# Transposes of the normed rows two token tiles later, and two units' first products ahead of the last transposes, in a hybrid encoder layer

## The chip, the core and the metric

One core of a Trainium2 chip runs the whole kernel. Its engines are TensorE (PE: matmuls and transposes; the loads of its stationary operand are shown as PEld), VectorE (DVE), ScalarE (ACT), GpSimd (POOL) and SyncE (SP, which here only issues DMAs). Each engine takes its instructions in order; semaphores tie the engines together. The metric is the device time of one execution in microseconds (us), as the median over runs.

## What is computed

One encoder layer on 2304 tokens (256 of a prompt and 2048 of a sample) with a model width of 1024: a norm, an input projection, an RWKV group and an attention group, an output projection, and a gated feed-forward net. The part that matters here is the end of the layer:

```
def rms_norm(x, g):
    y = xf * lax.rsqrt(jnp.mean(xf * xf, axis=-1, keepdims=True) + NORM_EPS)
    return (y * g.astype(jnp.float32)).astype(x.dtype)
...
    x = x + jnp.concatenate([y_rwkv, y_att], axis=-1) @ w_out
    h = rms_norm(x, norm2_g)
    x = x + (jax.nn.silu(h @ ffn_gate) * (h @ ffn_up)) @ ffn_down
    return x
```

The feed-forward width is 2816, that is 22 columns of 128. All data is fp32. A product of two fp32 operands is made of three matmuls: each operand is split into a high and a low part (`hi`, `lo`), and hi·hi, hi·lo and lo·hi are added up in PSUM.

## The kernel before, in words

The kernel runs the input projection, the RWKV phases and the attention first (the last store of the attention is issued at 2293.49 us of the profiled execution). Then `out_ffn` is called three times, for three blocks of 768 tokens, in the order 1, 0, 2 of `FF_ORDER`. It is the only function that the change touches. A block goes through these stages:

- Output projection, first half of the columns (0 to 511): six token tiles of 128 rows, 8 k-tiles each, `part` at lines 991 to 994; line 1000 adds the sum to the residual rows `xw`.
- Output projection, second half of the columns, one token tile after the other (loop over `j`, lines 1046 to 1071). One tile is 24 matmuls of 128x512 (lines 211 to 213). Its rows are then added to the residual (DVE, line 1050), stored (DMA on POOL's queue, line 1051), squared and summed (ACT, line 193), brought to the reciprocal root (POOL, lines 160 and 161), and multiplied by it and by the gain (DVE, line 1058). The result `h`, 128 tokens by 1024, is transposed on PE in 8 pieces of 128x128 (line 1062), because the feed-forward products need the width on the partitions, and ACT copies the pieces from PSUM (line 1063) into the four tiles `B` (names `cg` in the profile): two halves of the width by two halves of the tokens, each 128 x 4 x 384.
- The operands. The gate and up products are done with 7 products in place of 8 for each pair of columns: `b11` and `b21` are tiles of `B` as they are, `t1` to `t4` are differences of such tiles (`sub`, line 1073 and the following lines), and `b22` is the last tile. Each is split into `hi` (ACT) and `lo` (DVE) by `op` into two `H` buffers. `t1` and all later operands need all six token tiles; `b11` and `b21` need only the first three.
- 22 units (`units`): gate and up of 11 pairs of columns. A unit is 7 products of 12 matmuls of 128x384 (line 1087), with the operands b11, b21, t1, t2, b22, t3, t4 in this order. Its weights are two raw tiles of 128x1024 (`wsr`, loaded by SP), sums of their quarters (`sw`: POOL lines 1025 and 1035, DVE lines 1034 and 1039), and their splits (`wsh`, `wsl`, 4 buffers; `w2h`, `w2l`, 2 buffers). The generator `weights(u + 1)` is advanced one step after each product of unit `u`. The sum of products 1, 4 and 6 stays in one PSUM tile, which ACT copies out (lines 1113, 1122, 1128) before the next product is added to it; the copies go into `c`, one of the four `cg` buffers, so that the first unit's `c` has to wait until a tile of `B` is used up. 
- The down projection and the final norm.

The program is built with a scheduler that places the instructions of each engine by a model of its own; the order that a program really has is therefore shown as rows of the built program where it matters.

## Time and profile before

| | us |
|---|---|
| median of 3 runs (lowest to highest) | 4184.22 (4174.27 to 4196.87) |
| the profiled execution, its own time | 4194.28 |
| its span from the first to the last instruction | 4192.2 |
| PE busy | 3935.4 (94%) |
| DVE, ACT, POOL busy | 2867.8, 2010.2, 1252.0 |
| mean granted TensorE clock | 0.96 |

The clock is given as a share of 2.4 GHz; its two levels are 1.2 and 2.4 GHz. Times in the rows further down count from the start of the span. A row of the timeline gives the start, the length, the engine, the line, the operation, what is written and read, its size, how many equal instructions the row merges, and in brackets the idle time before it and what ended it. A row of a stretch gives its bounds and length, then for PE, PEld, DVE, ACT and POOL the busy time and the number of instructions, the granted clock, the share of the DMA engines' time and GB/s.

### The profile page before, as it was taken

To read this page: it belongs to the slowest core of one execution; us is meant where nothing else is said; L and a number is where in the kernel's file an instruction comes from. 1 tells how busy PE (TensorE), PEld (TensorE's weight loads), DVE (VectorE), ACT (ScalarE), POOL (GpSimd) and SP (SyncE) were. 2 spreads that over 40 slices of the span, in tenths; PEclk is the share of its full clock that TensorE was granted. 3 is DMA by queue.
4 is the path that set the end of the run, shared out by engine and by line. 5 is a ranking of instruction groups with operands and counts; after the bars stand their busy time and mean duration, and the time that the engine had idled before them with its cause. 6 is when DMAs were issued, how large, how long until landed. Compare 5 with 4: busy or idle time off the path is not lost.

```text
span 4192.2 us, 71175 instructions
## 1 busy us (share of the span) xinstructions
PE 3935.4 (94%) x26208; PEld 3379.6 (81%) x26208; DVE 2867.8 (68%) x4553; ACT 2010.2 (48%) x3940; POOL 1252.0 (30%) x1776
## 2 busy tenths in 40 slices
PE   8999999889999999999998789999799999799998
PEld 7987888657777787777775689988689988599987
DVE  5478686899889767898876377745377745377743
ACT  5354444456666555656665244434244433244432
POOL 2255353533233657443433012200122200112200
PEclk9999999879999999999999899999899999899999
DMA  6576566652434444444431323353223243222341
GB/s 202 164 213 210 182 209 197 203 139 46 113 68 99 103 107 113 104 109 111 108 83 48 123 96 101 96 182 122 109 91 106 103 174 130 96 100 102 101 171 70
DMA packets 646876, 524.32 MB, mean 125 GB/s; under 512 B 368512, under 2 KB 555520, under 8 KB 646528
## 3 DMA queue, kind: packets, MB, share of 16 engines
q1 hardware_dynamic: 577264, 438.36, 35.0%
q0 software_dynamic: 16944, 68.43, 4.9%
q10 hardware_dynamic: 52320, 12.98, 1.4%
q8 instruction: 207, 3.39, 0.3%
q14 instruction: 141, 1.16, 0.1%
HBM read 355.59 MB, written 166.37 MB: 125 GB/s over the span
## 4 chain that ended last, share of the span: by engine, by line
PE 78%; DVE 9%; POOL 3%; DMA 3%; issue 3%; ACT 3%; SPq 1%; ACTq 0%; DVEq 0%; POOLq 0%
PE acc L1087 23%; PE acc L211 9%; PE acc L212 9%; PE acc L213 9%; PE at L913 4%; PE g L657 3%; PE ao L917 3%; PE ao L916 3%; PE as L880 3%; PE as L881 2%; DVE nm L882 1%; DVE ptl L181 1%; PE hb L730 1%; PE hb L733 1%; PE hb L705 1%
## 5 line engine op out<-in xcount | busy, mean ns | idle before, releaser
L1087 PE MATMUL acc<-H,wsh 128*128 128x384 f32 x3168 | 814.5, 338 | 12.1 <-ACT cg L1113 12.1
L1087 PEld LDWEIGHTS acc<-H,wsh 128*128 128x128 f32 x3168 | 580.3, 191 | 13.4 <-ACT cg L1113 13.1
L1087 PE MATMUL acc<-H,wsl 128*128 128x384 f32 x1584 | 534.1, 337 | 0.0
L901 POOL TENSOR_SCALAR p<-p,f 128x512 f32<-128x512 f32 (+1 forms) x528 | 371.6, 725 | 287.9 <-DVE f L897 238.9
L211 PE MATMUL acc<-wsh,H 128*128 128x512 f32 x1080 | 432.8, 403 | 14.1 <-ACT wsh L175 14.1
L884 ACT ACTIVATE p<-as,nm 128x512 f32<-128x512 f32 (+1 forms) x528 | 360.5, 683 | 158.9 <-DVE nm L882 127.8
L212 PE MATMUL acc<-wsl,H 128*128 128x512 f32 x1080 | 431.1, 399 | 0.0
L213 PE MATMUL acc<-wsh,H 128*128 128x512 f32 x1080 | 425.8, 399 | 0.0
L175 ACT CAST pth<-at 128x512 fp32r<-128x512 f32 x520 | 299.7, 585 | 241.1 <-PE at L913 235.4
L181 DVE TENSOR_TENSOR ptl<-at,pth 128x512 fp32r<-128x512 f32 x520 | 353.0, 682 | 80.4 <-ACT pth L175 78.3
L882 DVE TENSOR_REDUCE nm<-as 128x1 f32<-128x512 f32 (+1 forms) x528 | 352.6, 673 | 77.4 <-PE as L881 74.8
L211 PE MATMUL acc<-hThi,wih 128*128 128x384 f32 x1008 | 351.5, 349 | 0.8 <-ACT hThi L175 0.7
L212 PE MATMUL acc<-hTlo,wih 128*128 128x384 f32 x1008 | 348.3, 346 | 0.0
L213 PE MATMUL acc<-hThi,wil 128*128 128x384 f32 x1008 | 348.0, 345 | 0.0
L913 PE MATMUL at<-ident,p 128*128 128x128 f32 x2080 | 329.5, 279 | 2.9 <-POOL p L901 2.5
L181 DVE TENSOR_TENSOR wsl<-wsr,wsh 128x1024 fp32r<-128x1024 f32 x156 | 193.0, 1237 | 195.1 <-ACT wsh L175 194.7
L175 ACT CAST wsh<-wsr 128x1024 fp32r<-128x1024 f32 x156 | 164.1, 1052 | 333.7 <-PE acc L213 162.3
L913 PEld LDWEIGHTS at<-ident,p 128*128 128x128 f32 x2080 | 264.7, 143 | 69.1 <-POOL p L901 5.6
L1087 PEld LDWEIGHTS acc<-H,wsl 128*128 128x128 f32 x1584 | 301.2, 190 | 0.0
L1025 POOL TENSOR_TENSOR sw<-wsr 128x512 f32<-128x512 f32 x66 | 84.8, 1285 | 691.2 <-DVE wsl L181 600.3
L880 PE MATMUL as<-kh,qs 128*128 128x512 f32 (+1 forms) x528 | 248.7, 471 | 31.2 <-ACT p L884 26.0
L211 PEld LDWEIGHTS acc<-wsh,H 128*128 128x128 f32 x1080 | 211.4, 196 | 59.1 <-ACT wsh L175 14.8
(661 smaller groups left out, 8379.7 us busy)
## 6 DMA issues: line engine op xcount, KB each, us to landing
wsr<-in_ffn_gate SPq DMA_DIRECT2D x66, 512.0 KB, 3.5
wsr<-in_ffn_up SPq DMA_DIRECT2D x66, 512.0 KB, 3.8
wsr<-in_ffn_down SPq DMA_DIRECT2D x66, 512.0 KB, 3.5
wir<-in_w_in POOLq DMA_DIRECT2D x63, 512.0 KB, 4.5
hd<-hid POOLq DMA_DIRECT2D x66, 384.0 KB, 3.7
H<-hd SPq DMA_DIRECT2D x33, 768.0 KB, 5.6
cl<-ard SPq DMA_DIRECT2D x144, 128.0 KB, 3.0
zT<-z SPq DMA_DIRECT2D x84, 192.0 KB, 2.7
```

Source lines behind the costliest of these rows:

```text
L175: nc.scalar.copy(out=hi, in_=src)
L181: e.tensor_tensor(out=lo, in0=src, in1=hi.bitcast(F32), op=ALU.subtract)
L211: mm(out, ahi, bhi, start=first, stop=False)
L212: mm(out, ahi, blo, start=False, stop=False)
L213: mm(out, alo, bhi, start=False, stop=last)
L657: nc.tensor.matmul(psgs[e][:, q, :], bk[rows, q, :], cl[rows, e, q, :], start=True, stop=True)
L880: nc.tensor.matmul(pss[:, :hw], qs[:, h, :], kh, start=True, stop=False)
L882: dve.tensor_reduce(out=nm[:, h, i:i + 1], in_=pss[:, :hw], axis=AX.X, op=ALU.max, negate=True)
L884: act.activation(out=p_[:, :hw], in_=pss[:, :hw], func=AF.Exp, bias=nm[:, h, i:i + 1], accum_out=ls[:, h, i:i + 1])
L901: pool.tensor_scalar(out=t, in0=t, scalar1=f[:, h, i:i + 1], scalar2=1.0, op0=ALU.mult, op1=ALU.mult)
L913: nc.tensor.transpose(tp[:, h, :], pt[h, i][:, k * P:(k + 1) * P], self.ident)
L1087: nc.tensor.matmul(acc, x[l][:, k, :], y_[r][:, k, :], start=first and k == 0 and i == 0, stop=k == 3 and i == 2, skip_group_check=True)
```

## The change

The diff keeps every matmul, transpose, split and sum of a block and changes their order and some buffers. The transposes of a tile become a function `turn(j)`. In the loop over the tiles `turn(j - 2)` is called after the product of tile `j`, so that the transposes of tile 0 stand behind the product of tile 2; `turn(4)` and `turn(5)` stand behind the loop. `h` now lies in one of the 14 `H` buffers and no longer in one of the four `wsr` buffers, and `load(1)` comes earlier. The unit becomes a class whose `steps()` is a generator with a stop after each product. Behind the loop the first two products of unit 0 (b11, b21) are called before `turn(4)` and `turn(5)`, and the first two of unit 1 before t2 is made; the weights of both units are advanced by hand in between. From unit 2 on the loop is as it was.

```
-            h = RAW()
+            h = HT([P, D], F32)
             dve.scalar_tensor_tensor(out=h, in0=xw[j], scalar=r, in1=g2, op0=ALU.mult, op1=ALU.mult)
-            for q in range(2):
-                tp = ACC().rearrange("p (i t) -> p i t", t=P)
-                for i in range(4):
-                    nc.tensor.transpose(tp[:, i, :], h[:, (q * 4 + i) * P:(q * 4 + i + 1) * P], self.ident)
-                act.copy(out=B[q][t][:, :, jj * P:jj * P + P], in_=tp)
-            if j == 2:
+            hs.append(h)
+            if j >= 2:
+                turn(j - 2)
+            if j == 3:
+                load(1)
+            if j == 4:
+                wts = [weights(0), weights(1)]
+                wt = [next(wts[0])]
                 op("b11", B[0][0])
                 op("b21", B[1][0])
-            if j == 3:
-                wg = weights(0)
-                for wt in wg:
-                    pass
-                load(1)
...
+        u0, u1 = Unit(0, wt[0]), None
+        p0 = u0.steps()
+        next(p0)
+        next(p0)
+        turn(4)
+        turn(5)
+        wt.append(next(wts[1]))
+        (b11, b12), (b21, b22) = B
+        sub = lambda out, x, y_: dve.tensor_tensor(out=out, in0=x, in1=y_, op=ALU.subtract)
+        sub(b11, b12, b11)
+        op("t1", b11)
+        next(wts[0])
+        next(wts[0])
+        u1 = Unit(1, wt[1])
+        u1.g = u0.c
+        p1 = u1.steps()
+        next(p1)
+        next(p1)
+        sub(b12, b22, b12)
+        sub(b11, b22, b11)
+        op("t2", b11)
+        next(p0)
+        next(wts[0])
+        op("b22", b22)
+        next(p0)
+        next(wts[0])
+        op("t3", b12)
+        sub(b21, b21, b11)
+        op("t4", b21)
+        next(wts[0])
+        for _ in p0:
+            next(wts[1], None)
+        load(2)
```

What the scheduler made of it is seen in the built programs. The first place is PE behind the last product of the second half, in the first block: `acc<-ident` are transposes (8 to a tile), L1087 of before and L1082 of the change are the units' products. Before:

```order
L213 MATMUL acc<-wsh,H 128x512
L1062 MATMUL acc<-ident,wsr 128x128 x8
L1087 MATMUL acc<-H,wsh 128x384 x2
L1087 MATMUL acc<-H,wsl 128x384
L1087 MATMUL acc<-H,wsh 128x384 x2
```

Now:

```order
L213 MATMUL acc<-wsh,H 128x512
L1054 MATMUL acc<-ident,H 128x128 x8
L1082 MATMUL acc<-H,wsh 128x384 x2
L1082 MATMUL acc<-H,wsl 128x384
L1082 MATMUL acc<-H,wsh 128x384 x2
L1082 MATMUL acc<-H,wsl 128x384
L1082 MATMUL acc<-H,wsh 128x384 x2
L1082 MATMUL acc<-H,wsl 128x384
L1082 MATMUL acc<-H,wsh 128x384 x2
L1082 MATMUL acc<-H,wsl 128x384
L1082 MATMUL acc<-H,wsh 128x384
L1054 MATMUL acc<-ident,H 128x128 x8
```

Before, the 8 transposes behind the last tile's product are that tile's own, and all products of the units follow. Now they are those of tile 3; a first product of unit 0 follows (its 12 matmuls, and one of the second product), then the transposes of tile 4, the rest of the second product, the transposes of tile 5, the two first products of unit 1, and then the third product of unit 0.

The second place is ACT from the last weights of the output projection on (`wsh<-wsr`, `w2h<-wsr`), in the first block; `junk,ss<-xw` is the squaring of a tile's rows, `cg<-acc` the copy of half of a tile's transposes.

```order
 L175 CAST wsh<-wsr 128x1024 x3
 L175 CAST w2h<-wsr 128x512
-L175 CAST wsh<-wsr 128x1024 x2
+L175 CAST wsh<-wsr 128x1024
+L175 CAST w2h<-wsr 128x512
+L175 CAST wsh<-wsr 128x1024
+L193 ACTIVATE junk,ss<-xw 128x1024 x2
+L1055 COPY cg<-acc 128x4x128
 L193 ACTIVATE junk,ss<-xw 128x1024
-L1063 COPY cg<-acc 128x4x128 x2
+L1055 COPY cg<-acc 128x4x128 x2
```

Two tiles are squared before the first copy of transposes, where one was; and the cast of unit 1's `w2h` now stands before the cast of the last weights of the output projection.

The third place is DVE from the last tile's multiplication by the gain to the low parts of t2, b22 and t3 (the row with x3), in the first block. `cg<-cg` are the differences of the operands, `H<-cg,H` low parts of operands, `wsl<-sw,wsh` low parts of weights, L1034 and L1039 sums of weights. Before:

```order
L1058 SCALAR_TENSOR_TENSOR wsr<-xw,rstd,gain 128x1024
L1073 TENSOR_TENSOR cg<-cg 128x1536 x2
L181 TENSOR_TENSOR H<-cg,H 128x1536
L1073 TENSOR_TENSOR cg<-cg 128x1536
L181 TENSOR_TENSOR wsl<-sw,wsh 128x1024
L1073 TENSOR_TENSOR cg<-cg 128x1536
L181 TENSOR_TENSOR H<-cg,H 128x1536 x3
```

Now:

```order
L1039 TENSOR_TENSOR sw<-wsr,sw 128x512
L1143 TENSOR_TENSOR cg<-cg 128x1536
L181 TENSOR_TENSOR wsl<-sw,wsh 128x1024
L1143 TENSOR_TENSOR cg<-cg 128x1536
L181 TENSOR_TENSOR H<-cg,H 128x1536
L181 TENSOR_TENSOR wsl<-sw,wsh 128x1024
L1143 TENSOR_TENSOR cg<-cg 128x1536
L1034 TENSOR_TENSOR sw<-sw,wsr 128x512
L1143 TENSOR_TENSOR cg<-cg 128x1536
L1039 TENSOR_TENSOR sw<-wsr,sw 128x512
L181 TENSOR_TENSOR H<-cg,H 128x1536 x3
```

Between the first difference and the low part of t2 there now stand two low parts of weights where there was one, and one pair of weight sums (L1034, L1039: those of unit 2). The pair of unit 1 stands between the last tile's multiplication and the first difference; before, it stood ahead of that multiplication. Ahead of the multiplication DVE now has the low parts of unit 0's and unit 1's first weights, of b11 and of b21. The other two blocks have the same order at these places.

## Rows read from the trace of the kernel before

**Rows 1.** The page, part 1: PE, busy time, share of the span, instructions.

```profile
PE 3935.4 (94%) x26208; PEld 3379.6 (81%) x26208; DVE 2867.8 (68%) x4553; ACT 2010.2 (48%) x3940; POOL 1252.0 (30%) x1776
```

**Rows 2.** Stretches of three blocks and one unit: length, engines' busy times, clock, DMA.

```profile
2347.40:2460.30 112.90, 79.39 (x336) 70.63 (x337) 55.27 (x51) 39.93 (x54) 17.14 (x24) 0.79 0.20 70
2969.40:3085.00 115.60, 81.85 (x336) 72.45 (x337) 55.14 (x51) 39.98 (x54) 17.09 (x24) 0.78 0.20 69
3594.00:3709.60 115.60, 81.53 (x337) 72.18 (x337) 55.29 (x51) 39.92 (x54) 17.10 (x24) 0.78 0.20 69
...
2445.80:2460.30 14.50, 14.50 (x85) 14.50 (x84) 9.49 (x13) 6.84 (x11) 2.54 (x2) 1.00 0.22 72
```

**Rows 3.** What PE waited for, 2338 to 3720 us: total, times, longest.

```profile
PE acc L1062 <- DVE wsr L1058: 89.2, 18, 8.0
PE acc L1087 <- ACT cg L1113: 12.1, 3, 4.0
```

**Rows 4.** Timeline of PE around the transposes of tile 0, first block.

```profile
2342.90 0.39 PE L213 MATMUL acc<-wsh,H 128*128 128x512 f32 x1
...
2346.98 0.39 PE L213 MATMUL acc<-wsh,H 128*128 128x512 f32 x1
2351.60 1.97 PE L1062 MATMUL acc<-ident,wsr 128*128 128x128 f32 x8 [4.23 <-DVE wsr L1058]
2353.22 0.78 PE L211 MATMUL acc<-wsh,H 128*128 128x512 f32 x1
```

**Rows 5.** Timelines of DVE, ACT and POOL: the way of tile 0 to `h`.

```profile
2347.41 0.69 DVE L1050 TENSOR_TENSOR xw<-acc,xw 128x512 f32<-128x512 f32 x1 [1.91 <-PE acc L213]
2348.13 1.06 ACT L193 ACTIVATE junk<-xw 128x1024 bf16<-128x1024 f32 x1 [5.11 <-DVE xw L1050]
2349.65 0.57 POOL L161 TENSOR_TENSOR rstd<-rstd,mhalf 128x1 f32<-128x1 f32 x1
2350.26 1.28 DVE L1058 SCALAR_TENSOR_TENSOR wsr<-xw,rstd,gain 128x1024 f32<-128x1024 f32 x1 [2.16 <-POOL rstd L161]
```

**Rows 6.** Timeline of PE: last transposes, first block; then t2's product.

```profile
2421.02 1.94 PE L1062 MATMUL acc<-ident,wsr 128*128 128x128 f32 x8 [7.97 <-DVE wsr L1058]
...
2434.95 1.01 PE L1087 MATMUL acc<-H,wsh 128*128 128x384 f32 x2 [4.05 <-ACT cg L1113]
...
2440.40 0.34 PE L1087 MATMUL acc<-H,wsl 128*128 128x384 f32 x1
```

**Rows 7.** Timeline of PE in the attention: transposes among other matmuls.

```profile
2289.64 0.60 PE L913 MATMUL at<-ident,p 128*128 128x128 f32 x4
```

**Rows 8.** Timelines of DVE and ACT: first difference to the copy before t2.

```profile
2422.76 3.62 DVE L1073 TENSOR_TENSOR cg<-cg 128x1536 f32<-128x1536 f32 x2 [1.89 <-ACT cg L1063]
...
2429.82 1.22 DVE L181 TENSOR_TENSOR wsl<-sw,wsh 128x1024 fp32r<-128x1024 f32 x1
...
2432.63 5.09 DVE L181 TENSOR_TENSOR H<-cg,H 128x1536 fp32r<-128x1536 f32 x3
...
2434.42 0.48 ACT L1113 COPY cg<-acc 128x384 f32<-128x384 f32 x1 [0.33 <-DVE H L181]
```

**Rows 9.** Timelines of POOL and DVE: unit 1's weight sums beside DVE's work.

```profile
2414.12 1.26 POOL L1025 TENSOR_TENSOR sw<-wsr 128x512 f32<-128x512 f32 x1 [11.71 <-DVE wsl L181]
2414.56 1.91 DVE L181 TENSOR_TENSOR wsl<-wsr,wsh 128x1024 fp32r<-128x1024 f32 x1
2415.34 2.24 POOL L1035 TENSOR_TENSOR sw<-wsr 128x512 f32<-128x512 f32 x1
2416.39 1.75 DVE L1034 TENSOR_TENSOR sw<-sw,wsr 128x512 f32<-128x512 f32 x1
2418.16 0.69 DVE L1039 TENSOR_TENSOR sw<-wsr,sw 128x512 f32<-128x512 f32 x1
```

**Rows 10.** DVE: last output weights' low part; page, part 6: loads of ffn_up.

```profile
2344.29 1.21 DVE L181 TENSOR_TENSOR wsl<-wsr,wsh 128x1024 fp32r<-128x1024 f32 x1
...
wsr<-in_ffn_up SPq DMA_DIRECT2D x66, 512.0 KB, 3.8
```

More of the change, by code (lines that the diff above doesn't have):

```diff
@@ L1045, in out_ffn, with turn @@
         load(0)
+        hs = []
+        def turn(j):
+            t, jj = j // 3, j % 3
+            for q in range(2):
+                tp = ACC().rearrange("p (i t) -> p i t", t=P)
+                for i in range(4):
+                    nc.tensor.transpose(tp[:, i, :], hs[j][:, (q * 4 + i) * P:(q * 4 + i + 1) * P], self.ident)
+                act.copy(out=B[q][t][:, :, jj * P:jj * P + P], in_=tp)
         for j in range(6):
@@ L1088, in product, with __init__, done, steps @@
                                      stop=k == 3 and i == 2, skip_group_check=True)
+        class Unit:
+            def __init__(self, u, wt):
+                self.up, self.wt = units[u][0] == "ffn_up", wt
+                self.A, self.B, self.D, self.E = (None,) * 4
+                self.c = sb.tile([P, 4, 384], F32, name="cg", tag="cg", bufs=4)
+            def done(self, i, x, fi, ti):
+                c = self.c[:, i, :]
+                dve.tensor_tensor(out=c, in0=x, in1=c, op=ALU.add)
+                if not self.up:
+                    th = sb.tile([P, 384], F32, name="th", tag="th", bufs=2)
+                    act.activation(out=th, in_=c, func=AF.Tanh, scale=0.5)
+                    dve.scalar_tensor_tensor(out=c, in0=th, scalar=1.0, in1=c, op0=ALU.add, op1=ALU.mult)
+                else:
+                    dve.scalar_tensor_tensor(out=self.hp[fi][:, ti * 384:ti * 384 + 384], in0=self.g[:, i, :], scalar=0.5,
+                                             in1=c, op0=ALU.mult, op1=ALU.mult)
+            def steps(self):
+                if self.up:
+                    self.hp = [sb.tile([P, 768], F32, name="hid", tag="xw", bufs=6) for _ in range(2)]
+                acc = lambda: ACC()[:, :384]
+                A, c, wt = acc(), self.c, self.wt
+                product(A, wt[0], ops["b11"], True)
+                act.copy(out=c[:, 0, :], in_=A)
+                yield
+                Bk = acc()
+                product(Bk, wt[1], ops["b21"], True)
+                self.done(0, Bk, 0, 0)
+                yield
+                Dk = acc()
+                product(Dk, wt[2], ops["t1"], True)
+                act.copy(out=c[:, 2, :], in_=Dk)
+                yield
+                product(A, wt[3], ops["t2"], False)
+                act.copy(out=c[:, 1, :], in_=A)
+                yield
+                product(Dk, wt[4], ops["b22"], False)
+                self.done(1, Dk, 0, 1)
+                yield
+                product(A, wt[5], ops["t3"], False)
+                act.copy(out=c[:, 3, :], in_=A)
+                self.done(2, A, 1, 1)
+                yield
+                E = acc()
+                product(E, wt[6], ops["t4"], True)
+                self.done(3, E, 1, 0)
+                yield
@@ L1125, in out_ffn @@
-            done(1, Dk, 0, 1)
-            wn = next(nw, wn)
-            product(A, s3, ops["t3"], False)
-            act.copy(out=c[:, 3, :], in_=A)
-            done(2, A, 1, 1)
-            wn = next(nw, wn)
-            product(E, a22, ops["t4"], True)
-            done(3, E, 1, 0)
+            if u == 1:
+                unit, pr = u1, p1
+                for _ in wts[1]:
+                    pass
+            else:
+                unit = Unit(u, wn)
+                unit.g = prev.c
+                pr = unit.steps()
@@ L1133, in out_ffn @@
+            wn = None
+            for _ in pr:
+                wn = next(nw, wn)
             for wn in nw:
                 pass
[L1135 to L1137 removed]
+            if unit.up:
+                ring[f] = unit.hp
                 for i in range(2):
[L1139 to L1140 removed]
+                    pool.dma_start(out=self.hd[b][f + i], in_=unit.hp[i])
+            prev = unit
         for j in range(6):
```

47 lines of the change are left out of this document (2 added, 45 removed).

## Prediction

> **What bounds the kernel now.** The page's first part is read first: PE is busy 94% of the span [rows 1], so time can come only from the places where PE waits or runs at the low clock. The change touches one kind of place, so the second view is the table of stretches. I cut one stretch in each block, from the end of tile 0's second-half product to the first product of unit 2. It is the same work before and after, and from unit 2 on the programs agree. The three stretches take 112.9, 115.6 and 115.6 us, together 344.1, with PE at 79 to 82 us of busy time and a granted clock of 0.78 to 0.79 [rows 2]. A unit behind them takes 14.5 us with PE full and the clock at 1.00 [rows 2]. So the stretch loses time in two ways, by waits and by the clock.
>
> The view of waits gives the first: in the three blocks together PE waited 89.2 us, 18 times, for the normed rows `h` ahead of transposes, and 12.1 us, 3 times, for ACT's copy ahead of t2's product [rows 3]. The timeline shows one such wait: tile 0's product issues its last matmul at 2346.98, the transposes start at 2351.60 after 4.23 us idle [rows 4]. The idle time is a chain over three engines: DVE's add, ACT's square, POOL's root, DVE's multiplication [rows 5]. The second loss is seen in the same place: after the wait the 8 transposes need 1.62 us to the next matmul (2351.60 to 2353.22) [rows 4], a pitch of 0.20, while four transposes among the attention's matmuls end 0.60 us after the first starts [rows 7], a pitch under 0.15. Half of the slow pitch is 0.10; I take 0.11, or 0.87 us for 8. And after the wait ahead of t2, 17 matmuls take 5.45 us (2434.95 to 2440.40) [rows 6] where at 14.5 / 84 = 0.173 [rows 2] they take 2.94: such a wait costs 2.5 us more in slow matmuls behind it.
>
> **The work that must remain on PE.** Tile matmuls at full clock have a pitch of (2346.98 - 2342.90) / 18 = 0.227 [rows 4], so a tile is 24 x 0.227 = 5.44 us, five tiles 27.2. Six sets of transposes are 5.2. The 14 products of units 0 and 1 are 2 x 14.5 = 29.0. Sum: 61.4 us a block. If no wait were left, a block would win 51.5 to 54.2 us and the kernel 160. That is the most the change can give.
>
> **The change part by part.** *Later transposes.* `h` of tile j is now wanted after two more tiles, 10.9 us after its product, and is ready 4.2 us after it [rows 4, 5]: hidden, with 6 us to spare, for tiles 0 to 3. PE has no wait from tile 1 to the transposes of tile 3, and the end of tile 5's product lies at 5 x 5.44 + 3 x 0.87 = 29.8 us from the start of the stretch.
>
> *First products of two units ahead of the last transposes.* Here DVE's queue decides, as its order in the built program shows. Tile 4's product ends at 4 x 5.44 + 2 x 0.87 = 23.5; its `h` follows 4.2 later, and 0.6 more since a copy of transposes stands ahead of the square on ACT: 28.3. From there DVE has no gap: low parts of weights 1.22 [rows 8], b11 1.7 (5.09 / 3) [rows 8], weights 1.22, tile 5's add 0.69 [rows 5], weights 1.22, b21 1.7, weights 1.22 make 9.0, and tile 5's multiplication 1.28 [rows 5] ends at 38.6. PE's second product of unit 0 cannot end before b21's low part, and the transposes of tile 5 not start before 38.6: I count 2.8 us of waiting on PE up to there, in place of the 7.97 us ahead of the last transposes [rows 6].
>
> *The sums of unit 1's weights* stand next on DVE. They need POOL's L1025, which starts when the last low part has freed its buffer, and takes 1.26; L1034 takes 1.75, L1039 0.69 [rows 9]. With the wait that is 38.6 + 1.3 + 1.75 + 0.69 = 42.3 for the first difference.
>
> *From the first difference to t2.* Before, this took from 2422.76 to the end of the first of the three low parts, 2432.63 + 1.70 = 2434.33: 11.6 us [rows 8]. Added to this run of DVE are one more low part of weights, 1.22, and unit 2's sums, 1.75 + 0.69 and 1.3 for its L1025: 5.0. So t2 is ready at 42.3 + 16.6 = 58.9, ACT's copy ends 0.5 later [rows 8], and t2's product starts at 59.6. PE meanwhile has only three products, so it waits some 14 us in this part, more than the 4.05 of before [rows 6]: most of what is left of the stall moves here, behind DVE.
>
> *The rest.* Nine products at 2.07 are 18.7, a short wait for t3 is 0.3, the slow matmuls after the long wait 2.5 as before. The stretch ends at 59.6 + 18.7 + 0.3 + 2.5 = 81.1 us.
>
> **POOL and DVE.** L1034 takes 1.75 us where L1039, of the same size, takes 0.69; the low part of weights beside L1025 takes 1.91 instead of 1.22, and L1035, started in that time, 2.24 [rows 8, 9]: the two engines hold each other up. I count 1.3 of waiting and 1.06 of lengthening for each of two pairs of sums, 4.7 us. The Trainium skill (SBUF — State Buffer, section "Who interferes with whom") says that a DVE instruction with two SBUF inputs and a GpSimd instruction that reads SBUF block each other wholly, whoever is first. By that rule all four POOL sums would be paid in DVE's queue, 4 x 1.26 = 5.0 us instead of 4.7, an estimate that would move the total by 1 us; rows 9 agree with it.
>
> **Costed at nothing.** `h` in an `H` buffer: eight are held by the output projection's left operands, five by `h` of tiles 0 to 4; those of tiles 0 to 2 are free after their transposes, before b11 and b21 need theirs. The DMAs are the same in number; without `h` in `wsr` unit 1's loads go out earlier. That moves the cast of unit 1's `w2h` ahead of the cast of the last output weights on ACT. The low part of those weights now starts at 2344.29 [rows 10]; a load issued when a buffer is freed lands 3.8 us later [rows 10], which I expect to delay it by 2 to 3 us. PE wants it later by about as much, since two k-steps of tile 1 now stand ahead of that use. Price: 0, at most 3 us a block if PE is first.
>
> **The sum.** Saved: 112.9 - 81.1 = 31.8, and 115.6 - 81.1 = 34.5 twice: 101 us. The profiled execution took 4194.3 us, so it becomes 4093; the median of the runs is 10 us below that execution, and I take the same saving from it: 4083 us.
>
> Bounds of the unknown sizes: if POOL's sums hide and the clock does not fall, 2.6 + 2.5 go and the block takes 76, the kernel 4068. If unit 2's and unit 0's elementwise work gets in DVE's way beyond my count, a second slow spell follows and the `w2h` load is late, a block takes up to 92 and the kernel 4116.
>
> **Rivals.**
> *DVE becomes the bound of the whole stretch (a smaller gain).* DVE is busy 55 us of the stretch [rows 2]; squeezed into 81 it is at 68%, and its in-order queue already sets three quarters of my end time. If late low parts also hold unit 2's first products, each block loses some 11 us more: 92 us, saved 21 + 24 + 24 = 68, time 4116. For it: the long queue above. Against it: unit 2's weights are wanted 20 us after t2 is ready.
> *The waits vanish as well (a larger gain).* DVE and ACT reach into the idle time of the tiles and PE waits less ahead of t2: 74 us a block, saved 122, time 4062. Against it: the differences need the last tile, and they are 11.6 us of DVE by themselves.
> *The clock stays low (slower).* If transposes between the tiles let the clock fall to 1.2 GHz and keep it there, the 61.4 us of PE work become 123, and with 10 us of waits a block takes 133: 18 us more on the mean than the 114.7 of now, 4184 + 55 = 4239. It decides when the low clock lasts for some 67 us a block, twice the 33.6 saved, almost all of the stretch's matmuls. For it: after every wait the transposes and the matmuls behind them ran slowly [rows 4, 6]. Against it: four transposes among matmuls ran at the short pitch [rows 7], and PE now has no wait before them. The Trainium skill (TensorE: Matmul & The Clock Gate, section "Part 4: PE-mode transpose") states that a transpose does not count as PE activity in the same way as a matmul; rows 7 show no loss from it when matmuls stand on both sides.
> *The change does nothing*: if the transposes did not set the end. Rows 3 and 4 are against it, since PE idles there with nothing else in its queue.
>
> **How the numbers follow.** My forecast (4068 to 4100) has a chance of 0.60, the larger gain 0.13, the smaller gain 0.20 (4100 to 4135), the slow clock 0.03, no effect 0.04. The predicted time is that of the forecast. The range leaves out the ends of the two gain rivals, the slow clock and no effect: 4056 to 4120. Half a per cent, 21 us, is about what a measurement of this kernel can tell from no change: faster 0.93, the same 0.04, slower 0.03.
>
> **What the profile after would show.** Right: PE has no wait ahead of the transposes of tiles 0 to 3, the clock stays at 1.00 over the tiles; the longest wait of the stretch, 8 to 10 us, stands ahead of t2's product behind ACT's copy, a second of 4 to 5 us around t1's; the stretch is some 81 us long. Wrong: a wait ahead of the transposes of tiles 1 to 3, unit 2 starting late behind `wsl`, PE waiting for the last output weights at tile 0, or a clock under 0.9 over the tiles.

## The result, and the profile after

The changed kernel takes 4085.9 us (median of 4 runs, 4076.95 to 4088.94) where the kernel before took 4190.55 in the same comparison: ratio 0.9752, 95% interval 0.9717 to 0.9787. The forecast was 4083 us in a range of 4056 to 4120.

A stretch is counted from the 168th matmul of a block's output projection (in the kernel before that is the end of tile 0's second-half product) to the first product of unit 2, so it holds the same work in every kernel here. The windows of the three stretches after, with the columns of [rows 2]:

```profile
2336.67:2415.10 78.43, 65.62 (x337) 59.38 (x336) 54.49 (x51) 37.59 (x53) 19.58 (x24) 0.93 0.24 87
2924.13:3003.94 79.81, 67.01 (x337) 60.80 (x336) 53.97 (x50) 37.69 (x53) 19.53 (x24) 0.91 0.24 86
3512.98:3592.00 79.02, 65.87 (x337) 59.22 (x337) 53.98 (x50) 37.40 (x53) 19.53 (x24) 0.91 0.23 84
sum 237.26, PE 198.50 PEld 179.40 DVE 162.44 ACT 112.68 POOL 58.63; mean PE 66.17 PEld 59.80 DVE 54.15 ACT 37.56 POOL 19.54
```

The three took 344.1 us before, so 106.9 us went here. DVE has the same 54 to 55 us of work as before; PE's busy time fell from some 81 us to 66, because more of its work runs at the full clock. The profiled spans differ by more, 4192.2 - 4074.8 = 117.4 us. The rest arose ahead of the feed-forward part, which the change does not touch: the first block's stretch starts at 2336.67 here, at 2347.40 before, and at 2348.49 in a second profile of the same changed kernel (below), whose span is 4087.6. Over the profiles of all kernels below this start scatters from 2336.67 to 2360.62.

What PE waited for over the three stretches, with the columns of [rows 3]:

```profile
PE acc L1082 <- ACT cg L1110: 23.0, 3, 8.0
PE acc L1082 <- DVE H L181: 9.3, 6, 2.5
PE acc L1054 <- DVE H L1068: 6.2, 3, 2.1
PE acc L1082 <- ACT H L175: 0.3, 1, 0.3
```

89.2 us ahead of transposes, in 18 waits, have become 6.2 in 3, those of tile 5. The wait for ACT's copy ahead of t2's product has grown from 12.1 to 23.0. The timeline of PE shows where they stand in the first block (L1054 are transposes, L1082 the units' products):

```profile
2366.43 1.03 PE L1054 MATMUL acc<-ident,H 128*128 128x128 f32 x8
2367.22 0.69 PE L1082 MATMUL acc<-H,wsh 128*128 128x384 f32 x2
...
2372.00 0.44 PE L1082 MATMUL acc<-H,wsh 128*128 128x384 f32 x1 [1.29 <-DVE H L181]
...
2376.24 1.06 PE L1054 MATMUL acc<-ident,H 128*128 128x128 f32 x8 [2.06 <-DVE H L1068]
...
2384.70 0.45 PE L1082 MATMUL acc<-H,wsh 128*128 128x384 f32 x1 [1.48 <-DVE H L181]
...
2394.86 1.01 PE L1082 MATMUL acc<-H,wsh 128*128 128x384 f32 x2 [7.98 <-ACT cg L1110]
```

The transposes of tile 3 start without a wait, 29.8 us after the start of the stretch, and eight of them take 0.79 us to the next matmul (1.62 in [rows 4]). After that come four waits: b21's low part, tile 5's `h`, t1, t2.

The same stretch cut where tile 4's transposes start and at t2's product:

```profile
2336.67:2369.84 33.17, 33.17 (x167) 28.09 (x167) 15.56 (x16) 15.64 (x24) 7.23 (x16) 1.00 0.29 111
2369.84:2394.86 25.02, 12.21 (x65) 11.05 (x62) 23.10 (x17) 11.91 (x16) 9.81 (x7) 0.86 0.24 84
2394.86:2415.10 20.24, 20.24 (x109) 20.24 (x109) 15.84 (x20) 10.04 (x16) 2.54 (x2) 0.92 0.16 53
```

In the first part PE is never idle. In the middle 25 us it works half the time, and DVE works 23.1 of 25.0. PE's four waits there, 1.29 + 2.06 + 1.48 + 7.98 = 12.8 us, all end behind rows of DVE, the last by way of ACT's copy: what is left of the stall lies in DVE's queue. Its rows there, and those of POOL and ACT:

```profile
2373.81 2.29 DVE L1068 SCALAR_TENSOR_TENSOR H<-xw,rstd,gain 128x1024 f32<-128x1024 f32 x1 [0.73 <-POOL rstd L161]
2376.02 1.75 DVE L1034 TENSOR_TENSOR sw<-sw,wsr 128x512 f32<-128x512 f32 x1
2377.81 0.69 DVE L1039 TENSOR_TENSOR sw<-wsr,sw 128x512 f32<-128x512 f32 x1
2378.42 1.75 DVE L1143 TENSOR_TENSOR cg<-cg 128x1536 f32<-128x1536 f32 x1
...
2385.70 1.75 DVE L1143 TENSOR_TENSOR cg<-cg 128x1536 f32<-128x1536 f32 x1
2388.61 1.75 DVE L1034 TENSOR_TENSOR sw<-sw,wsr 128x512 f32<-128x512 f32 x1 [1.16 <-POOL sw L1025]
2390.28 1.75 DVE L1143 TENSOR_TENSOR cg<-cg 128x1536 f32<-128x1536 f32 x1
2391.95 0.68 DVE L1039 TENSOR_TENSOR sw<-wsr,sw 128x512 f32<-128x512 f32 x1
2392.55 5.08 DVE L181 TENSOR_TENSOR H<-cg,H 128x1536 fp32r<-128x1536 f32 x3
```

```profile
2371.49 1.65 POOL L160 TENSOR_SCALAR rstd<-ss 128x1 f32<-128x1 f32 x1 [1.44 <-ACT junk L193]
...
2373.75 1.26 POOL L1025 TENSOR_TENSOR sw<-wsr 128x512 f32<-128x512 f32 x1
...
2385.86 2.71 POOL L1025 TENSOR_TENSOR sw<-wsr 128x512 f32<-128x512 f32 x1 [8.63 <-DVE wsl L181]
```

```profile
2387.48 4.22 ACT L175 CAST H<-cg 128x1536 fp32r<-128x1536 f32 x3 [3.46 <-DVE cg L1143]
2394.33 0.48 ACT L1110 COPY cg<-acc 128x384 f32<-128x384 f32 x1 [2.63 <-DVE H L181]
```

The difference for t2 is done at 2387.4, and ACT has its high part, the first of three, at about 2388.9 (2387.48 + 4.22 / 3). But its low part starts at 2392.55: unit 2's sums (L1034, L1039) and the last difference stand ahead of it in DVE's queue.

### The profile page after: what moved, and what is told of

It reads as the page before. It is cut to its first block, busy times and chain, and to the rows that moved or that the text cites. A ratio compares the mean times of both kernels' runs of the same rounds, so it can differ in the third digit from the quotient of the medians.

```text
span 4074.8 us, 71176 instructions
## 1 busy us (share of the span) xinstructions
PE 3880.8 (95%) x26208; PEld 3336.7 (82%) x26208; DVE 2866.1 (70%) x4553; ACT 2005.5 (49%) x3940; POOL 1257.7 (31%) x1776
## 3 DMA queue, kind: packets, MB, share of 16 engines
q14 instruction: 141, 1.16, 0.1%
## 4 chain that ended last, share of the span: by engine, by line
PE 76%; DVE 9%; DMA 4%; POOL 4%; issue 3%; ACT 3%; SPq 1%; ACTq 0%; DVEq 0%; POOLq 0%
PE acc L1082 23%; PE acc L211 8%; PE acc L212 8%; PE acc L213 8%; PE at L913 5%; PE g L657 3%; PE ao L917 3%; PE ao L916 3%; PE as L880 3%; PE as L881 2%; DVE nm L882 1%; DVE ptl L181 1%; PE hb L705 1%; PE hb L730 1%; PE g L597 1%
## 5 line engine op out<-in xcount | busy, mean ns | idle before, releaser
L1082 PE MATMUL acc<-H,wsh 128*128 128x384 f32 x3168 | 814.6, 337 | 32.6 <-ACT cg L1110 23.0
L1082 PEld LDWEIGHTS acc<-H,wsh 128*128 128x128 f32 x3168 | 578.7, 190 | 36.2 <-ACT cg L1110 24.1
L1082 PE MATMUL acc<-H,wsl 128*128 128x384 f32 x1584 | 533.2, 337 | 0.0
L211 PE MATMUL acc<-wsh,H 128*128 128x512 f32 x1080 | 419.8, 391 | 14.6 <-ACT wsh L175 14.6
L212 PE MATMUL acc<-wsl,H 128*128 128x512 f32 x1080 | 420.6, 390 | 0.0
L213 PE MATMUL acc<-wsh,H 128*128 128x512 f32 x1080 | 415.6, 389 | 0.0
L882 DVE TENSOR_REDUCE nm<-as 128x1 f32<-128x512 f32 (+1 forms) x528 | 353.0, 674 | 75.2 <-PE as L881 72.7
L913 PE MATMUL at<-ident,p 128*128 128x128 f32 x2080 | 326.5, 277 | 2.9 <-POOL p L901 2.5
L1082 PEld LDWEIGHTS acc<-H,wsl 128*128 128x128 f32 x1584 | 300.4, 190 | 0.0
L1025 POOL TENSOR_TENSOR sw<-wsr 128x512 f32<-128x512 f32 x66 | 89.2, 1352 | 643.8 <-DVE wsl L181 552.8
L181 DVE TENSOR_TENSOR wsl<-sw,wsh 128x1024 fp32r<-128x1024 f32 x132 | 161.2, 1221 | 138.3 <-ACT wsh L175 138.1
```

Source lines behind the costliest of these rows:

```text
L181: e.tensor_tensor(out=lo, in0=src, in1=hi.bitcast(F32), op=ALU.subtract)
L211: mm(out, ahi, bhi, start=first, stop=False)
L212: mm(out, ahi, blo, start=False, stop=False)
L213: mm(out, alo, bhi, start=False, stop=last)
L882: dve.tensor_reduce(out=nm[:, h, i:i + 1], in_=pss[:, :hw], axis=AX.X, op=ALU.max, negate=True)
L913: nc.tensor.transpose(tp[:, h, :], pt[h, i][:, k * P:(k + 1) * P], self.ident)
```

## The experiments

The theory of the prediction: the wait for `h` is hidden by the later transposes, and what is left is set by DVE's queue between tile 4's `h` and t2. The main rival: the products ahead of the last transposes are what covers the waits. All results, the stretches taken from the windows of each run:

| kernel | ratio to before, 95% interval | stretches, us | sum | t2's product starts, us |
|---|---|---|---|---|
| before | 1 | 112.9, 115.6, 115.6 | 344.1 | 90.2 |
| the change | 0.9752 (0.9717 to 0.9787) | 78.4, 79.8, 79.0 | 237.3 | 58.2 |
| the change, again | 0.9744 (0.9717 to 0.9770) | 81.3, 78.7, 78.5 | 238.5 | 58.2 |
| only later transposes | 0.9749 (0.9735 to 0.9764) | 81.6, 81.0, 81.1 | 243.7 | 55.5 |
| only products ahead | 0.9973 (0.9963 to 0.9982) | 107.4, 110.3, 108.8 | 326.5 | 89.0 |
| one tile later | 0.9766 (0.9747 to 0.9786) | 82.4, 81.6, 81.6 | 245.6 | 61.3 |
| low parts first | 0.9739 (0.9712 to 0.9766) | 80.3, 78.4, 78.3 | 236.9 | 57.0 |
| POOL's sums on DVE | 0.9726 (0.9699 to 0.9753) | 77.8, 77.1, 76.0 | 230.9 | 55.9 |
| both of these | 0.9717 (0.9691 to 0.9743) | 77.5, 75.5, 76.7 | 229.7 | 55.3 |
| unit 2's sums later | 0.9726 (0.9711 to 0.9740) | 79.9, 78.1, 78.0 | 236.0 | 56.8 |
| tile 5 first | 0.9776 (0.9752 to 0.9801) | 84.1, 81.9, 81.7 | 247.7 | 60.9 |
| by need | 0.9722 (0.9701 to 0.9742) | 78.3, 75.3, 75.2 | 228.8 | 54.9 |
| by need, sums on DVE | 0.9712 (0.9699 to 0.9725) | 74.9, 74.4, 74.6 | 223.9 | 53.2 |
| the same, nothing ahead | 0.9741 (0.9722 to 0.9761) | 79.4, 77.8, 77.8 | 234.9 | 53.2 |

The intervals are 2 to 7 thousandths wide, 8 to 30 us, so the runs from "low parts first" on are told apart by their stretches rather than by their times. The two profiles of the changed kernel agree within 1.1 us in the second and third stretch, and differ by 2.9 in the first. The last column counts from the start of the stretch, in the second block. It repeats better than the stretch: the third block gives the same within 0.1 us in all changed kernels but two ("only later transposes" 0.3, "only products ahead" 1.5). What lies behind t2's product varies more: 20.2 us in the first block of the change, and in the other two, with PE never idle either:

```profile
2982.30:3003.94 21.64, 21.64 (x108) 21.64 (x109) 15.84 (x20) 10.15 (x16) 2.54 (x2) 0.86 0.16 49
3571.15:3592.00 20.85, 20.85 (x109) 20.85 (x110) 15.85 (x20) 9.95 (x16) 2.54 (x2) 0.89 0.16 51
```

The longer it takes, the lower is the granted clock (0.92, 0.89, 0.86), so a difference of a microsecond in one stretch can be the length of this slow spell alone.

**The change once more**, to see how far its stretches repeat.

> The changed kernel once more, unchanged, on the chip of the three runs beside it. Its stretches were 78.6, 79.9 and 79.2 us. If the stretches are what the change moves and the rest varies from run to run, they come out within 0.5 us of that, ratio to before 0.975.

Two of three stretches came lower by 0.6 and 1.1 us, the first higher by 2.9; the sum moved by 1.2 us, so 0.5 us was too narrow. (The expectation's 78.6, 79.9 and 79.2 are the 78.4, 79.8 and 79.0 of the table, between rounded edges.) In the first block of this profile PE waits 0.32 and 1.04 us for the last output weights, the transposes of tile 3 start 31.7 us after the start of the stretch instead of 29.8, and the part behind t2's product is 1.0 longer: together the 2.9 us.

**Only the later transposes.** The kernel before, with `turn` as in the change and both last sets of transposes ahead of every product:

```diff
-            h = RAW()
+            h = HT([P, D], F32)
...
+            hs.append(h)
+            if j >= 2:
+                turn(j - 2)
...
+            if j == 4:
+                op("b11", B[0][0])
+                op("b21", B[1][0])
+        turn(4)
+        turn(5)
+        wg = weights(0)
+        for wt in wg:
+            pass
```

> Only the first half of the change: transposes two tiles later, all six sets ahead of any product of a unit. Theory of the prediction (the hidden wait for h carries nearly all, DVE's queue sets what is left): no wait ahead of the transposes of tiles 0 to 4; h of tile 5 comes out of DVE's queue some 41 us after the end of tile 0's product, so PE waits about 9 us ahead of the last transposes; but unit 2's weight sums are not in DVE's run to t2, t2 is ready at about 56 us, and eleven products and the slow start behind it bring the stretch to 82 us (78.6 to 79.9 with the whole change). Kernel 8 us above the changed one, ratio to before 0.977. Rival (the products ahead of the last transposes are what covers the waits of the last two tiles and of t1 and t2): both waits come back as before, 8 and 4 us, on top of 79: 91 us a stretch, ratio 0.984.

Measured 81.2 us a stretch, the theory's 82 and not the rival's 91. The ratio is 0.9749 where the theory had 0.977; by its time this kernel can't be told from the whole change. PE's timeline in the second block (L1097 is the product here):

```profile
2978.35 1.97 PE L1054 MATMUL acc<-ident,H 128*128 128x128 f32 x8 [9.71 <-DVE H L1068]
...
2992.50 1.01 PE L1097 MATMUL acc<-H,wsh 128*128 128x384 f32 x2 [4.04 <-ACT cg L1123]
```

The wait ahead of the last transposes is back (9.71, where the change has 2.06), but the one ahead of t2 is 4.04 instead of 7.98. The products ahead fill the first wait and then are missing before t2. Besides, t2's product starts at 55.5 us here and at 58.2 in the change, whose DVE has more to do on the way to it. So 100.4 of the 106.9 us come with the later transposes alone.

**Only the products ahead.** The change with `turn(j)` behind tile `j`:

```diff
-            if j >= 2:
-                turn(j - 2)
+            if j < 4:
+                turn(j)
```

> Only the second half: the first products of two units stay ahead of the transposes of tiles 4 and 5, but tiles 0 to 3 are transposed right behind their own product. Theory of the prediction: the four waits for h of 4 to 5 us are back, each with slow transposes behind it, about 6.5 us a tile, so 26 us; DVE has more idle time before tile 5 and gives about 4 back. Stretch 101 us, ratio to before 0.990. Rival (the products ahead are the larger half): stretch at most 88 us, ratio 0.981 or less.

Measured 108.8 us, 17.6 us saved in all three stretches; the rival falls. By the ratio it is 11 us; in part that is because just ahead of the first stretch PE waits 1.97 and 2.20 us for the last output weights, which in the kernel before it doesn't. This kernel also has `h` in an `H` buffer and the earlier `load(1)`, so these are not what brings the bulk of the gain. The theory's 101 is missed as well: the four tiles cost what was expected (transposes start 13.1 us apart in the first block, against 6.3 in the change), but nothing came back from DVE's idle time. PE waits 14.3 us in the three blocks for ACT's high parts (0.3 in the change). And the low parts of weights and of b11, b21 still follow tile 4's `h`; beside them POOL's root of tile 5, a 128x1 operation that takes 0.18 us elsewhere, can take long (second block):

```profile
3038.24 1.75 DVE L181 TENSOR_TENSOR H<-cg,H 128x1536 fp32r<-128x1536 f32 x1
3039.90 2.35 DVE L181 TENSOR_TENSOR wsl<-sw,wsh 128x1024 fp32r<-128x1024 f32 x2
3042.18 1.75 DVE L181 TENSOR_TENSOR H<-cg,H 128x1536 fp32r<-128x1536 f32 x1
3044.66 2.31 DVE L1068 SCALAR_TENSOR_TENSOR H<-xw,rstd,gain 128x1024 f32<-128x1024 f32 x1 [0.73 <-POOL rstd L161]
```

```profile
3033.31 0.18 POOL L160 TENSOR_SCALAR rstd<-ss 128x1 f32<-128x1 f32 x1 [0.52 <-ACT junk L193]
...
3040.89 3.09 POOL L160 TENSOR_SCALAR rstd<-ss 128x1 f32<-128x1 f32 x1 [1.66 <-ACT junk L193]
```

In the first block, beside the same operations of DVE, it took 0.28 us:

```profile
2423.05 0.28 POOL L160 TENSOR_SCALAR rstd<-ss 128x1 f32<-128x1 f32 x1 [1.66 <-ACT junk L193]
```

That stretch is 107.4 us, against 110.3 and 108.8 with 3.09, so the slow root is only a small part of what the theory missed.

**One tile later instead of two.** `if 1 <= j <= 4: turn(j - 1)` in the change.

> The whole change, but the transposes of tiles 0 to 3 follow one tile later instead of two. Theory of the prediction: h is ready 4.2 us after its product and a tile takes 5.4, so one tile hides it too; stretch 79 us within 1, ratio to before 0.975. Rival (the second tile is needed, because ACT's copies of transposes and POOL's root come late between the tiles): waits of 0.5 to 1.5 us ahead of four sets and a low clock behind them, 83 to 86 us, ratio 0.979.

Measured 81.9 us: 2.6 more than the mean of the change's two profiles, short of the rival's 83 to 86. PE waits once ahead of tile 0's transposes (second block):

```profile
2945.12 1.09 PE L1054 MATMUL acc<-ident,H 128*128 128x128 f32 x8 [1.98 <-DVE H L1068]
```

```profile
2940.46 0.69 DVE L1060 TENSOR_TENSOR xw<-acc,xw 128x512 f32<-128x512 f32 x1 [3.21 <-PE acc L213]
2943.18 0.69 DVE L1060 TENSOR_TENSOR xw<-acc,xw 128x512 f32<-128x512 f32 x1 [2.03 <-PE acc L213]
```

In the second block the first two tiles overlap on PE, so their products end 2.7 us apart and not 5.4, and one tile does not hide the 4.2 us of the chain; in the first block this wait is 1.26 us. Ahead of the transposes of tiles 1 to 3 there is no wait, so against waits the second tile of distance is needed at the start of the block only. But `h` of tile 4 comes 3.1 us later than in the change (31.0 against 27.9 us after the start of the stretch): besides the wait of 2.0, one more set of transposes, 0.8 us, now stands ahead of tile 4's product.

**Low parts first.** `issue_after(x)` queues what is written under it behind `x` on `x`'s engine; `ops["t3"][2]` is the instruction of t3's low part.

```diff
-        sub(b21, b21, b11)
+        with self.tc.issue_after(ops["t3"][2]): sub(b21, b21, b11)
...
-                wn = next(nw, wn)
+                with self.tc.issue_after(ops["t3"][2]): wn = next(nw, wn)
```

> The changed kernel, with DVE's last difference and unit 2's weight sums queued behind the low parts of t2, b22 and t3. Theory (DVE's order between t1 and t2 sets the longest wait): the low part of t2 starts when ACT has its high part, 3.7 us earlier than in the changed kernel, and PE's wait ahead of t2 falls from 8.0 to about 4.3 us; stretch 75.5 us, 11 us in all, ratio to before 0.9725. Rival (what is pushed back is late next): t4 or unit 2's weights make PE wait about as much later; stretch 79 us, ratio 0.975.

Measured 79.0, the rival's number, but not by its mechanism: behind t2's product PE is never idle. t2's product starts 1.2 us earlier than in the change (57.0 against 58.2), where 3.7 were expected. The low part did start earlier against its difference, 2991.17 - 2987.88 = 3.3 us after it instead of 2392.55 - 2385.70 = 6.9. But ACT's copy, which PE waits for, came late (DVE and ACT, second block):

```profile
2991.17 5.78 DVE L181 TENSOR_TENSOR H<-cg,H 128x1536 fp32r<-128x1536 f32 x3 [1.54 <-ACT H L175]
```

```profile
2995.31 0.48 ACT L1110 COPY cg<-acc 128x384 f32<-128x384 f32 x1 [1.43 <-DVE H L181]
```

It starts 4.1 us after the first low part begins, so behind the second of the three; in the change it starts 1.8 us after (2392.55 and 2394.33). Its target `c` needs one of the four `cg` buffers. t2's source is also read by the last difference, which now stood later, so this buffer was not free behind t2's low part, and the copy's time fits the next operand's. This is argued, since the trace doesn't name the buffer; the next run puts the difference back.

**Unit 2's sums later, the last difference as in the change.** Only the second pair of lines of that diff.

> The changed kernel with only unit 2's weight sums behind the low parts of t2, b22 and t3; the last difference stays ahead of them. Theory (in the run that queued the last difference behind them too, the gain was lost because the buffer of the copy ahead of t2's product came free later): t2's low part starts 3.6 us earlier and the copy with it, PE's wait ahead of t2 falls from 8.0 to 4.4 us, stretch 75.7 us, ratio to before 0.972. Rival (given back again by b22, t3 or the low clock): 78 us or more, ratio 0.974.

Measured 78.7 us, the rival's number. Of the theory's step a part was there: t2's product starts 1.4 us earlier than in the change, not 3.6 (second block):

```profile
2983.47 4.51 DVE L1143 TENSOR_TENSOR cg<-cg 128x1536 f32<-128x1536 f32 x2
2987.90 6.17 DVE L181 TENSOR_TENSOR H<-cg,H 128x1536 fp32r<-128x1536 f32 x3
```

```profile
2983.62 2.73 POOL L1025 TENSOR_TENSOR sw<-wsr 128x512 f32<-128x512 f32 x1 [8.63 <-DVE wsl L181]
2986.31 2.80 POOL L1035 TENSOR_TENSOR sw<-wsr 128x512 f32<-128x512 f32 x1
```

ACT's copy now starts at 2990.76, 2.9 us after the start of the low parts and right behind the first. Only the place of the last difference is changed against the run before, so that is what moved the copy; this bears out the buffer. But the two differences took 4.51 us where two take 3.55 elsewhere, and the low parts 6.17 where three take 5.08: beside POOL's two sums for unit 2, which the edit did not move, they cost 2.05 us more, and 3.6 less 2.05 is about the 1.4 that was left. In the change DVE waited for L1025 in its queue; with that wait gone, the sums lengthen the instructions that it runs in their place.

**POOL's sums on DVE**, for units 1 and 2:

```diff
-            pool.tensor_tensor(out=s[:, 0, :], in0=a21, in1=a22, op=ALU.add)
+            (dve if u in (1, 2) else pool).tensor_tensor(out=s[:, 0, :], in0=a21, in1=a22, op=ALU.add)
...
-            pool.tensor_tensor(out=s[:, 3, :], in0=a11, in1=a21, op=ALU.subtract)
+            (dve if u in (1, 2) else pool).tensor_tensor(out=s[:, 3, :], in0=a11, in1=a21, op=ALU.subtract)
```

> The changed kernel, with the sums of the weights of units 1 and 2 that POOL makes moved to DVE. Theory (POOL and DVE hold each other up): the sum at L1034 takes 0.69 instead of 1.75 us and tile 5's multiplication 1.28 instead of 2.29, no wait for POOL; four sums of 0.69 more on DVE. By the order of DVE's queue t2's low part comes 1.4 us earlier; stretch 78 us, ratio to before 0.974. Rival (L1034 is slow by its own operands): it stays at 1.75, DVE's queue grows by four sums less the waits, and the stretch becomes 80.5 us, ratio 0.976.

Measured 77.0, by the theory (78) and not the rival (80.5), and the rows are its rows (second block):

```profile
2980.30 1.28 DVE L1068 SCALAR_TENSOR_TENSOR H<-xw,rstd,gain 128x1024 f32<-128x1024 f32 x1 [0.73 <-POOL rstd L161]
...
2982.71 0.69 DVE L1034 TENSOR_TENSOR sw<-sw,wsr 128x512 f32<-128x512 f32 x1
```

Tile 5's multiplication takes 1.28 instead of 2.29, L1034 0.69 instead of 1.75. DVE does 2.8 us more of sums in a block (4 x 0.69) and the block is 2.3 shorter. t2's low part starts at 2996.34, 53.2 us after the start of the stretch, 2.7 earlier than in the change, where the theory had 1.4; 0.7 of the difference is unit 2's L1039, which went behind that low part.

**Both edits together** (low parts first, POOL's sums on DVE).

> Both edits together. Theory: the 3.7 us of the low parts and about 1 us of the first pair of sums add up; wait ahead of t2 about 4 us, stretch 74.5 us, ratio to before 0.972. Rival (after one of them another bound is reached, PE's own work of 61.4 us and the slow spell behind the wait, or b22 and t3): as the better of the two alone, 75.5 us.

Measured 76.6 us, 0.4 better than the sums alone, which is the rival's "as the better of the two alone" in kind, if not its 75.5; t2's product starts at 55.3 us, with the sums alone at 55.9. ACT's copy again starts 3.5 us after the first low part begins, behind the second of the three, as in the run with the low parts first.

**Tile 5 first.** b21 is split behind the loop; `last` is tile 5's multiplication:

```diff
-                op("b21", B[1][0])
...
         next(p0)
+        turn(4); turn(5)
+        with self.tc.issue_after(last): op("b21", B[1][0])
         next(p0)
-        turn(4)
-        turn(5)
-        wt.append(next(wts[1]))
+        with self.tc.issue_after(last): wt.append(next(wts[1]))
```

The second and the third of the four splits of unit 0's weights are queued behind `last` in the same way.

> The changed kernel with tile 5's rows ahead of other work: on DVE the low parts of b21, of unit 1's first and of unit 0's later weights queue behind tile 5's multiplication, and the transposes of tiles 4 and 5 stand ahead of unit 0's second product. h of tile 5 comes 4 us earlier. Theory (DVE's total work between tile 4's h and t2 sets the end, about 30 us of which none is taken away): the work that stood ahead of the multiplication now stands behind it, t2 is no earlier, stretch 79 us within 1, ratio to before 0.974. Rival (the lateness of tile 5 sets the end): all later steps move up by 4 us, stretch 75 us, ratio 0.971.

Measured 82.6 us: the rival falls, and the theory's number was too low. The rows of DVE, second block:

```profile
2971.25 1.29 DVE L1068 SCALAR_TENSOR_TENSOR H<-xw,rstd,gain 128x1024 f32<-128x1024 f32 x1 [3.46 <-POOL rstd L161]
...
2995.05 3.41 DVE L181 TENSOR_TENSOR H<-cg,H 128x1536 fp32r<-128x1536 f32 x2
```

`h` of tile 5 is ready 36.1 us after the start of the stretch (39.4 in the change), and still t2's low part begins 2.7 us later (58.6 against 55.9): DVE now waits 3.46 us for POOL's root with its other work queued behind, where it waited 0.73, and that difference is the 2.7. What bounds is the sum of DVE's work up to t2, and an idle DVE adds to it.

**By need.** Tile 5 first, and the sums of units 1 and 2 behind the low part of t3 (unit 2's as in "low parts first"; unit 1's here):

```diff
         for _ in p0:
-            next(wts[1], None)
+            with self.tc.issue_after(ops["t3"][2]): next(wts[1], None)
```

> As the run with tile 5's rows first, and unit 1's and unit 2's weight sums queue behind the low parts of t2, b22 and t3 as well. Theory: about 6 us of DVE's work leave the way to t2, and tile 5's earlier h is of use now; t2's product starts 5 to 6 us earlier than in the changed kernel, stretch 73.5 us, ratio to before 0.970. Rival (unit 1's third product then waits for its sums): 77 us, ratio 0.973.

Measured 75.3 and 75.2 us in two blocks and 78.3 in the first, 76.3 in the mean: in number nearer to the rival (77) than to the theory (73.5). But the rival's wait of unit 1 isn't there, PE is never idle behind t2's product. The theory's step came smaller: t2's product starts at 54.9 us, 3.3 earlier than in the change and not 5 to 6. With less work in DVE's way to t2 the same early tile 5 is of use. Beside POOL's sums the first two differences took 5.61 us where two take 3.55 (second block), which is 2.1 of what is missing:

```profile
2980.65 5.61 DVE L1143 TENSOR_TENSOR cg<-cg 128x1536 f32<-128x1536 f32 x2
```

**By need, with POOL's sums on DVE.**

> As the run before it, with POOL's sums for units 1 and 2 made by DVE. Theory (POOL's sums stop DVE for as long as they last): the low parts and differences to t2 are no longer held up, at the price of one sum of 0.69 us in that run; 1 to 1.5 us earlier, stretch 72 us, ratio to before 0.969. Rival (with the order by need POOL's sums fall beside DVE's idle time): the same as without, or 0.7 us longer.

Measured 74.6 us in the mean, 4.7 below the change's two profiles, and 4075.3 us in the median: the lowest of all these kernels, 10.6 us below the changed kernel by medians of separate comparisons. The intervals of the two ratios overlap, so it is the stretches that show the gain. The first two differences, each 1.75 us now, and the sum between them take 4.0 us where the two took 5.61 (second block):

```profile
2968.72 1.75 DVE L1143 TENSOR_TENSOR cg<-cg 128x1536 f32<-128x1536 f32 x1
2970.38 0.69 DVE L1025 TENSOR_TENSOR sw<-wsr 128x512 f32<-128x512 f32 x1
2970.99 1.75 DVE L1143 TENSOR_TENSOR cg<-cg 128x1536 f32<-128x1536 f32 x1
```

t2's product starts 53.2 us after the start of the stretch there, 54.9 with POOL's sums. Of these 1.7 us this stretch keeps 0.9: behind t2's product it takes 21.2 us at a granted clock of 0.88, where it was 20.4 at 0.92.

**The same, with nothing ahead of the transposes.** `turn(4)` and `turn(5)` before the first product, unit 1's first two products behind unit 0's last.

> The kernel ordered by need with POOL's sums on DVE, but without the products ahead: all transposes stand before unit 0's first product, and unit 1's first two products stand behind unit 0's last. DVE's order up to the low part of t3 is the same, so t2 is ready at the same time, 53 us after the start of the stretch. Theory (the products ahead fill PE's wait for DVE, and are worth their own length once DVE's order no longer pays for them): two products more stand behind t2, 4.2 us, stretch 78.7 us instead of 74.6, ratio to before 0.974. Rival (they are worth only what they brought in the changed kernel, some 2 us a block): 76.6 us, ratio 0.9725.

Measured 78.3 us, 3.7 more, nearer to the theory (78.7) than to the rival (76.6). t2's product starts at the same 53.2 us (2982.09 in the second block). So the products ahead are worth nearly their length here. In the change they are worth some 2 us: there t2's product starts 2.7 us later than with the later transposes alone (58.2 against 55.5), which takes back most of their 4.2.

## Why the prediction was right

*Later transposes.* Right, and the bulk of the gain. No wait up to the transposes of tile 3; tile 5's product ends at 29.8 us, as forecast; eight transposes take 0.79 us where 0.87 was counted. The granted clock is 1.00 over the 33.17 us in which 32 of a block's 48 transposes of `h` and all tile matmuls behind tile 0's lie, and over the same part of the other two blocks, so the rival of the slow clock is out. The rule of the Trainium skill that the prediction weighed against it (TensorE: Matmul & The Clock Gate, section "Part 4: PE-mode transpose", a transpose does not count as PE activity in the same way) brought no loss here, with matmuls on both sides of every eight.

*Tile 5.* Forecast 38.6 us for its `h`, measured 39.4. The reason given was wrong in part: DVE's queue was not gapless. The multiplication waited 0.73 us for POOL's root, which took 1.65 us instead of 0.18 beside DVE's low parts, and was itself held up by POOL's L1025 (2.29 instead of 1.28). The forecast had no term for the root's delay. PE waits 1.29 + 2.06 = 3.35 us there, forecast 2.8.

*From there to t2.* The first difference starts at 41.8 (forecast 42.3), t2's product at 58.2 (59.6), by the queue as forecast. The wait of 1.3 us for unit 1's first POOL sum did not come: L1034 follows the multiplication without a gap, and the sum's price shows in the longer multiplication. PE's waits in it were put at 14 us and are 1.48 + 7.98 = 9.5: the step that was mis-sized. Three products were counted at 6.2 us; with tile 5's transposes and slow matmuls behind the wait PE's work there is 9.3 us. It did not move the end, because DVE sets it. The second wait was expected at 4 to 5 us and is 1.5 to 2.5; the longest, expected at 8 to 10, is 7.0 to 8.0.

*Behind t2.* 20.2, 21.6 and 20.9 us in the three blocks, 20.9 in the mean, instead of 21.5. Together 79.1 us a stretch where 81.1 was forecast, 106.9 us saved instead of 101. By the medians of the comparison 104.7 us were saved. The kernel before has the same three runs there as in the forecast and one more, of 4197.11 us, which moves its median from 4184.22 to 4190.55. That the time came out only 3 us from the forecast is in part luck: 4 us more saved stand against 6 us more to start from.

*POOL and DVE.* 4.7 us a block were counted. In the rows of the change the multiplication is 1.01 longer, the two L1034 1.06 each, and the wait is 1.16: 4.3. The run with the sums on DVE gives 2.3 (shorter) + 2.8 (paid for four sums) - 0.7 (one L1039 that went behind t2's low part) = 4.4. By the rule of the Trainium skill (SBUF — State Buffer, section "Who interferes with whom") the estimate was 5.0; 4.3 and 4.4 lie nearer to the count, but the difference is too small to decide.

*Unit 1's `w2h`.* Priced at 0, at most 3 us. In the profile of the change there is no wait for the last output weights, but that profile is an exception: in 11 of the 13 profiles of changed kernels PE waits 0.4 to 1.0 us for their low part in the first stretch, and t2's product starts 0.7 to 2.1 us later there than in the second; in a twelfth, with only the products ahead, the wait lies just ahead of the stretch. The other two blocks, and the kernel before, don't show it. So the price is 1 to 2 us in one block of three, and the sign of being wrong that the prediction named (PE waiting for the last output weights) is there in a small size.

*What the prediction did not see.* It summed both halves of the change into one number. The experiments show that the later transposes bring 100 us by themselves (in the stretches), and the products ahead 11 to 18 by themselves but only some 6 on top of them: they move PE's work from behind t2 to before tile 5, where DVE then is as late for t2 as it was for tile 5. The rival "DVE becomes the bound" named the mechanism of what is left; it did not reach unit 2, as the sum assumed.

Two things stay open: why the first block of one profile escaped the wait for the last output weights, and how much of the 4.2 us wait ahead of t2 in the kernel ordered by need, with the sums on DVE, could still be filled.

## What to carry to other kernels

Where PE waits for a chain over three engines after every tile, using the chain's result two tiles later took the wait and the slow matmuls behind it away together; PE's busy time fell by some 15 us a block at the same work, which is two fifths of the 35.6 us gained, and the rest is idle time. Work pulled ahead to fill a wait paid 2 us a block where the engine that PE waits for was also given the preparation of that work, and 3.7 where it was not: sum that engine's queue up to the next operand, and put what is needed later behind it. Before moving an instruction, look who else reads its buffer and what runs on POOL at that moment.

## What was not expected of the hardware

A 128x1 operation on POOL (L160) takes 0.18 us when DVE is idle, and 1.65 (the change), 2.57 (one tile later) and 3.09 us (only products ahead) while DVE runs operations with two SBUF inputs back to back; once, beside the same operations, it took 0.28. In the longest case it ended at 3043.98, when the last of three such instructions ended (3042.18 + 1.75), and not between them. Such a small step in a chain can cost more than the large ones; in the kernel ordered by need, where DVE is idle at that moment, it is 0.18 again. The other way round, POOL's sums lengthened DVE's instructions: two differences of 3.55 us took 4.51 and 5.61.

The clock behind equal waits differed. Tile 5's transposes start after 2.06 to 2.07 us of waiting in each block of the change, and over the next 4.3 to 4.8 us the granted clock was 0.64 (2376.24 to 2381), 0.60 (2963.68 to 2968) and 1.00 (3552.53 to 3557). It did not move t2's product, which DVE's queue sets.
